# A state-space stage: the products of states take their natural place, and a chunk's state comes ahead of its diagonal products

## The chip, the core and the metric

The kernel runs on one core of one Trainium2 chip. The metric is the device time of that core in microseconds (us), from the first to the last instruction and the little that lies around them. A core has engines that work side by side, each on its own queue, in the order in which the program wrote it: TensorE (PE) multiplies matrices, VectorE (DVE) and ScalarE (ACT) and GpSimd (POOL) work element by element, SyncE (SP) issues transfers. An instruction at the head of a queue that waits for another engine holds up all that stands behind it in that queue.

## What is computed

The reference is two blocks of a network on 512 positions of 1024 channels. The change touches one part of the second block, a state-space mixer. Its input projection gives z, x, B, C and dt; 32 heads of 64 channels stand in 4 groups of 8 heads, and each group goes over 4 chunks of 128 positions, carrying a state from chunk to chunk:

```
def step(state, inp):
    xc, ac, bc, cc = inp
    acum = jnp.cumsum(ac, axis=1)
    seg = jnp.where(causal, acum[:, :, None] - acum[:, None, :], -jnp.inf)
    scores = jnp.einsum('btgn,bsgn->btsg', cc, bc)[..., None] * jnp.exp(seg)
    y_diag = jnp.einsum('btsgh,bsghp->btghp', scores, xc)
    y_off = jnp.einsum('btgn,bghpn->btghp', cc, state) * jnp.exp(acum)[..., None]
    w_end = jnp.exp(acum[:, -1:] - acum)
    new_state = (state * jnp.exp(acum[:, -1])[..., None, None]
                 + jnp.einsum('bsgn,bsghp->bghpn', bc, xc * w_end[..., None]))
    return new_state, y_diag + y_off
```

A gate with z, a norm over each group and the output projection follow. All sums are in fp32.

## The kernel before

The state-space stage lies at about 740 to 1005 us of the span. Its main work is the projections: 128x512 products into PSUM tiles named pa. Operands that need it are split in a rounded part (hi) and a rest (lo), and each product is then three matmuls, hi by hi, hi by lo and lo by hi (mm3, lines 328, 329, 330). These matmuls into pa tiles are called fill here. The scan of a group is woven in among the fill of the next projection; the fourth group stands in the last projection of z, and its end in the output projection.

The scan of group g is the function ssd(g), made of steps on chunks c = 0 to 3:

- rows: two transfers (line 1264, issued by SP, 1 MB each) bring the running sums of the group's eight heads to all partitions, as tiles M.
- scores: four matmuls (line 1243) of B by C, and a copy by ACT (line 1245).
- bt: B is transposed on PE (line 1254) and split in hi and lo (1256 on ACT, 1257 on DVE); C is split too (1248 on ACT, 1249 on POOL).
- decay(i), for each of eight heads: a triangular mask on POOL (line 1272), four exponentials on ACT (1275, one for each chunk), and a product with the scores on DVE (1277). They work on M in place.
- xs(c): four transposes on PE (1284), then on DVE x times dt (1286) and x times D (1287); for c < 3 POOL weighs the former to the end of the chunk (xw, line 1291), ACT rounds it (1248) and POOL forms the rest (1249). The last two are the function parts.
- diag(c): 16 short matmuls (line 1301; the trace has 32 records for them) of M by x, and an addition on DVE (1306).
- state(c), c < 3: three matmuls (328 to 330, into a tile named ps) of B by xw. For c = 0 ACT copies the result (1324); for c > 0 POOL multiplies the old state by its decay (1326) and DVE adds (1328). Then parts splits the new state (1248 on ACT, 1249 on POOL).
- off(c), c > 0: three matmuls (328 to 330, into ps) of C by the parts of state c-1, a product on DVE (1313), an addition on POOL (1315).
- gate, factor, norm, trans: lines 1335, 1340 onwards, 1347, 1353 and 1354.

The matmuls of state, off and diag go to PSUM tiles ps, of which there are four; fill has four pa.

What sets the order on each engine: the program is written as a list of steps s, spread evenly among the steps of the projection by run. A scheduler then orders the instructions of each engine as their operands come free by its own reckoning, and among those that are ready by a priority, which is the place in the program moved forward by a number from the table PRIO. A step is wrapped whole in the priority of its name (L, through at and prio): "state" is 420, "off" is -10, "decay" -860, "xs" -15; the diagonal matmuls have "diag_mm", 3000. The numbers are kept by the change.

## Time and profile before

| | |
|---|---|
| three runs, median (lowest to highest) | 1377.48 us (1375.86 to 1381.73) |
| the profiled execution, its own time | 1378.86 us |
| its span (first to last instruction) | 1377.1 us |
| mean granted TensorE clock, as a share of full speed | 0.988 |
| PE busy | 1316.9 us (96%) |
| DVE, ACT, POOL busy | 862.8 (63%), 659.0 (48%), 311.5 us (23%) |

Busy shares are means over the whole span. A row of the timeline tells when an instruction, or a run of like ones (x and their number), began, how long it lasted, and in brackets how long its engine had been idle just before it and which instruction released it. The matmuls are pipelined: one lasts 0.39 us by its record, while the next begins 0.23 us behind it.

### The profile page before, as it was taken

What the parts mean: (1) busy time and instruction counts of PE and PEld (TensorE: products, weight loads), DVE (VectorE), ACT (ScalarE), POOL (GpSimd) and SP (SyncE); (2) the same over time, 40 slices, a digit from 0 to 9 for tenths busy, and PEclk for the clock granted to TensorE, in tenths of its full rate; (3) what the DMA queues carried; (4) which work ended last, traced back from release to release, by engine and by line L of the source; (5) the groups of instructions that cost most, each with busy time, mean ns of one, the idle gap of its engine ahead of it and who ended that gap; (6) DMA issues with size and microseconds to landing.
All of it is one profiled execution on the core that took longest, in us unless ns stands there. A gap on an engine that the chain in (4) does not pass through costs nothing. (4 is left out here: it accounts for less than half of the span.)

```text
span 1377.1 us, 20584 instructions
## 1 busy us (share of the span) xinstructions
PE 1316.9 (96%) x7927; PEld 1029.5 (75%) x7927; DVE 862.8 (63%) x1260; ACT 659.0 (48%) x1211; POOL 311.5 (23%) x321
## 2 busy tenths in 40 slices
PE   8998999989999999999999999999899999999997
PEld 5773666768888888888778777777688787777776
DVE  5734874294355544422868889677844966777865
ACT  5422464264222223312768465667542835555543
POOL 3532322031000000000202443342400412433421
PEclk9999999999999999999999999999999999999999
DMA  9787663015366654233258354414124354232311
GB/s 298 200 229 209 190 223 101 18 46 185 117 219 214 214 187 135 87 106 118 55 159 278 103 195 149 145 47 161 32 93 138 107 168 123 77 97 72 96 43 61
DMA packets 134733, 189.10 MB, mean 137 GB/s; under 512 B 10280, under 2 KB 95556, under 8 KB 133612
## 3 DMA queue, kind: packets, MB, share of 16 engines
q1 hardware_dynamic: 134588, 187.79, 44.5%
q8 instruction: 62, 1.02, 0.3%
q14 instruction: 35, 0.29, 0.1%
q10 hardware_dynamic: 48, 0.01, 0.0%
HBM read 178.25 MB, written 3.24 MB: 132 GB/s over the span
## 5 line engine op out<-in xcount | busy, mean ns | idle before, releaser
L273 DVE TENSOR_TENSOR wlo<-raw,whi 128x1024 fp32r<-128x1024 f32 (+1 forms) x160 | 208.8, 1316 | 219.2 <-ACT whi L269 209.2
L269 ACT CAST whi<-raw 128x1024 fp32r<-128x1024 f32 (+1 forms) x177 | 182.8, 1046 | 292.2 <-PE pa L329 121.6
L328 PE MATMUL pa<-b,whi 128*128 128x512 f32 x744 | 299.0, 402 | 0.0
L329 PE MATMUL pa<-b,whi 128*128 128x512 f32 x744 | 298.8, 402 | 0.0
L330 PE MATMUL pa<-b,wlo 128*128 128x512 f32 x744 | 297.4, 400 | 0.0
L329 PE MATMUL pa<-wlo,b 128*128 128x512 f32 x424 | 166.6, 393 | 3.4 <-DVE sm L581 3.0
L328 PE MATMUL pa<-whi,b 128*128 128x512 f32 x424 | 166.8, 395 | 1.9 <-ACT b L90 1.5
L330 PE MATMUL pa<-whi,b 128*128 128x512 f32 x424 | 166.1, 393 | 0.0
L328 PEld LDWEIGHTS pa<-b,whi 128*128 128x128 f32 x744 | 140.8, 189 | 32.5 <-issue 6.1
L330 PEld LDWEIGHTS pa<-b,wlo 128*128 128x128 f32 x744 | 140.8, 189 | 31.9 <-issue 1.9
L329 PEld LDWEIGHTS pa<-b,whi 128*128 128x128 f32 x744 | 141.0, 190 | 29.5 <-issue 0.5
L505 DVE SCALAR_TENSOR_TENSOR acc<-raw,c,acc 128x1024 f32<-128x1024 f32 x84 | 118.1, 1406 | 66.4 <-DMA raw<-in_ada_w_dram 44.3
L681 POOL TENSOR_TENSOR b<-w,b 128x512 fp32r<-128x512 f32 x24 | 36.1, 1519 | 469.3 <-DVE sm L586 288.0
L329 PEld LDWEIGHTS pa<-wlo,b 128*128 128x128 f32 x424 | 80.0, 189 | 20.7 <-DVE wlo L273 3.7
L328 PEld LDWEIGHTS pa<-whi,b 128*128 128x128 f32 x424 | 80.2, 189 | 19.2 <-issue 1.8
L330 PEld LDWEIGHTS pa<-whi,b 128*128 128x128 f32 x424 | 79.9, 188 | 17.4 <-issue 0.6
L1457 DVE TENSOR_TENSOR_SCAN w<-w,own 128x512 f32<-128x512 f32 (+3 forms) x64 | 64.1, 1046 | 15.6 <-ACT w L1454 15.6
L1459 POOL TENSOR_TENSOR w<-w,w 128x511 f32<-128x511 f32 (+3 forms) x64 | 67.8, 1063 | 21.8 <-DVE w L1457 20.9
L328 PE MATMUL ps<-whi,b 128*128 128x512 f32 x184 | 72.2, 393 | 0.0
L329 PE MATMUL ps<-wlo,b 128*128 128x512 f32 x184 | 72.1, 392 | 0.0
L330 PE MATMUL ps<-whi,b 128*128 128x512 f32 x184 | 71.9, 391 | 0.0
L777 PE MATMUL ps<-ident,w 128*128 128x128 f32 x240 | 53.5, 283 | 6.1 <-ACT w L787 4.0
(356 smaller groups left out, 2151.8 us busy)
## 6 DMA issues: line engine op xcount, KB each, us to landing
raw<-in_ada_w_dram SPq DMA_DIRECT2D x80, 512.0 KB
raw<-in_w_ffn_in_dram SPq DMA_DIRECT2D x44, 512.0 KB
raw<-in_m_in_w_dram SPq DMA_DIRECT2D x40, 512.0 KB
raw<-in_w_ffn_out_dram SPq DMA_DIRECT2D x22, 512.0 KB
b<-in_ada_w_dram SPq DMA_DIRECT2D x16, 512.0 KB
raw<-in_kv_ada_w_dram SPq DMA_DIRECT2D x16, 512.0 KB
b<-cumd SPq DMA_DIRECT2D x8, 1024.0 KB
raw<-in_m_out_w_dram SPq DMA_DIRECT2D x16, 512.0 KB
```

Source lines behind the costliest of these rows:

```text
L269: nc.scalar.copy(hi[:, :n], u.raw)
L273: eng.tensor_tensor(lo[:, :n], u.raw, hi[:, :n].bitcast(F32), ALU.subtract)
L328: mm(ps, lhsT=lh, rhs=rh, start=first, stop=False)
L329: mm(ps, lhsT=lh, rhs=rl, start=False, stop=False)
L330: mm(ps, lhsT=ll, rhs=rh, start=False, stop=last)
L505: nc.vector.scalar_tensor_tensor(acc, raw, ck, acc, ALU.mult, ALU.add)
L681: nc.gpsimd.tensor_tensor(lo, y[i], hi.bitcast(F32), ALU.subtract)
L777: nc.tensor.transpose(ps[:, (t - s) * P : (t - s + 1) * P], Ps()[e][t][:, s * P : (s + 1) * P], self.ident)
L1457: nc.vector.tensor_tensor_scan(R[:, 0:N][:, ::-1], R[:, 0:N][:, ::-1], self.own[:, S - N : S][:, ::-1], 0.0, ALU.mult, ALU.max)
L1459: nc.gpsimd.tensor_tensor(pr_[:, : N - 1], pr_[:, : N - 1], R[:, 1:N], ALU.mult)
```

## The change

Two things are changed in ssd. First, state and off are no longer wrapped whole in their priority: the PSUM tile and the three matmuls keep the place in which the program writes them, and only what empties the tile (copy or decay, addition, parts for state; product and addition for off) has the priority of that name. Second, the list of steps is written in another order: state(0) stood two places ahead of the end of the decays and now comes behind xs(1); and for each chunk the order is xs(c+1), state(c), diag(c), off(c), where it was xs(c+1), diag(c), off(c), state(c).

```diff
@@ off(c)
                 self.mm3(po, t[:, 2, cs_[c]], t[:, 3, cs_[c]], *box["sp", c - 1], True, True)
-                yo = self.w512()
-                nc.vector.tensor_tensor(r3(yo), r3(po), q(2, c), ALU.mult)
-                y = box["y"][:, c, :]
-                nc.gpsimd.tensor_tensor(y, y, yo, ALU.add)
+                with self.prio("off"):
+                    yo = self.w512()
+                    nc.vector.tensor_tensor(r3(yo), r3(po), q(2, c), ALU.mult)
+                    y = box["y"][:, c, :]
+                    nc.gpsimd.tensor_tensor(y, y, yo, ALU.add)
@@ state(c)
                 self.mm3(pu, t[:, 0, cs_[c]], t[:, 1, cs_[c]], *box["xw", c], True, True)
-                new = box["st", c] = self.w512()
-                box["sp", c] = [self.w512(F32R), self.w512(F32R)]
-                if c == 0:
-                    nc.scalar.copy(new, pu)
-                else:
-                    nc.gpsimd.tensor_tensor(r3(new), r3(box["st", c - 1]), hb(dec[:, 32 * c + 8 * g : 32 * c + 8 * g + 8]),
-                                            ALU.mult)
-                    nc.vector.tensor_tensor(new, pu, new, ALU.add)
-                parts(new, *box["sp", c])
+                with self.prio("state"):
+                    new = box["st", c] = self.w512()
+                    box["sp", c] = [self.w512(F32R), self.w512(F32R)]
+                    if c == 0:
+                        nc.scalar.copy(new, pu)
+                    else:
+                        d = dec[:, 32 * c + 8 * g : 32 * c + 8 * g + 8]
+                        nc.gpsimd.tensor_tensor(r3(new), r3(box["st", c - 1]), hb(d), ALU.mult)
+                        nc.vector.tensor_tensor(new, pu, new, ALU.add)
+                    parts(new, *box["sp", c])
@@ the order of the steps
             L = lambda f, *a: self.at(f.__name__, [lambda: f(*a)])[0]
+            M = lambda f, *a: lambda: f(*a)
             s = [L(rows, 0), L(rows, 1), L(scores), L(bt), L(xs, 0)] + [L(decay, i) for i in range(8)]
-            s.insert(-2, L(state, 0))
+
             for c in range(NT):
                 if c + 1 < NT:
-                    s += [L(xs, c + 1)]
+                    s += [L(xs, c + 1), M(state, c)]
                 s += [L(diag, c)]
                 if c > 0:
-                    s += [L(off, c)]
-                if 0 < c < NT - 1:
-                    s += [L(state, c)]
+                    s += [M(off, c)]
```

No instruction of the four compute engines is added or taken away but two loads of ACT's tables fewer (43 before, 41 after, in the program as it is written). What moves is the order on each engine. Behind line 1310 the line numbers of the changed kernel are up to two or three higher: its copy of state 0 is line 1326, the decay of a state 1329, the addition 1330, the transposes of trans 1355.

The first place is the middle of group 1 on PE, from the transposes of xs(3) on. Before, three products of fill stand between those (tile ps_7328) and the diagonal matmuls of chunk 2 (tile ps_7343):

```order
L1284 MATMUL ps_7328<-ident,b_6623 128x128 x4
L329 MATMUL pa_7406<-b_5508,whi_7203 128x512
L330 MATMUL pa_7406<-b_5506,wlo_7204 128x512
L328 MATMUL pa_7406<-b_5506,whi_7203 128x512
L1301 MATMUL ps_7343<-w_7242,b_6911 64x64 x8
L1301 MATMUL ps_7343<-w_7242,b_6920 64x64 x8
```

After, the three matmuls of state(2) (tile ps_7343, from w_7248 and w_7249, the hi and lo parts of xw) stand ahead of the diagonal ones of chunk 2 (tile ps_7360):

```order
L328 MATMUL pa_7470<-b_5505,whi_7124 128x512
L328 MATMUL ps_7343<-w_7248,b_6947 128x512
L329 MATMUL pa_7470<-b_5507,whi_7124 128x512
L330 MATMUL pa_7470<-b_5505,wlo_7125 128x512
L329 MATMUL ps_7343<-w_7249,b_6947 128x512
L330 MATMUL ps_7343<-w_7248,b_6947 128x512
L328 MATMUL pa_7470<-b_5505,whi_7124 128x512
L329 MATMUL pa_7470<-b_5507,whi_7124 128x512
L330 MATMUL pa_7470<-b_5505,wlo_7125 128x512
L1301 MATMUL ps_7360<-w_7242,b_6911 64x64 x8
L1301 MATMUL ps_7360<-w_7242,b_6920 64x64 x8
```

Before, state(2) came ten products of fill and one of off(2) behind the diagonal matmuls of chunk 2, so that state(2) has moved ahead of those and of some nine products of fill; the matmuls of off(2), which stood around it, now stand by themselves behind the diagonal ones.

The second place is the start of group 3 on PE, where the scores (line 1243) are formed among the last transposes of group 2 (line 1353). Before, they stand among the fill that makes tile pa_8370 from the weights whi_8205:

```order
L330 MATMUL pa_8370<-whi_8205,b_5507 128x512
L1353 MATMUL ps_8326<-ident,b_7740 128x128
L1353 MATMUL ps_8338<-ident,b_7740 128x128
L1243 MATMUL ps_8374<-b_6001 128x128 x4
L1353 MATMUL ps_8338<-ident,b_7740 128x128
L328 MATMUL pa_8370<-whi_8205,b_5505 128x512
```

After, they stand among the fill from the weights whi_8317, the next ones but one:

```order
L1355 MATMUL ps_8326<-ident,b_7740 128x128 x4
L328 MATMUL pa_8359<-whi_8317,b_5506 128x512
L1355 MATMUL ps_8338<-ident,b_7740 128x128
L1243 MATMUL ps_8374<-b_6001 128x128 x4
L1355 MATMUL ps_8338<-ident,b_7740 128x128 x3
L329 MATMUL pa_8359<-wlo_8318,b_5506 128x512
```

The first diagonal matmuls of group 3 stand behind the same product of fill in both orders. Between the scores and them lay 87 products of fill, and now lie 47: the scores moved 40 products back. In the other groups these counts are 111 and 111 (group 0), 105 and 99 (group 1), 115 and 114 (group 2).

The third place is ACT in the same stretch of group 3. Before, the copy of state 0 (line 1324) has five of the group's 32 exponentials behind it:

```order
L1248 CAST w_8414<-w_8412 128x512
L1275 ACTIVATE b_8368<-b_8368,w_6053 128x128 x5
L1324 COPY w_8501<-ps_8497 128x512
L269 CAST whi_8632<-raw_8321 128x1024
L1248 CAST w_8502<-w_8501 128x512
L1275 ACTIVATE b_8368<-b_8368,w_6053 128x128 x5
L1248 CAST w_8552<-w_8550 128x512
L269 CAST whi_8748<-raw_8357 128x1024
L1140 ACT_TABLE_LOAD
```

After, the copy (line 1326) has 24 of the 32 behind it:

```order
L1248 CAST w_8414<-w_8412 128x512
L1275 ACTIVATE b_8363<-b_8363,w_6053 128x128 x6
L1248 CAST w_8539<-w_8537 128x512
L269 CAST whi_8636<-raw_8321 128x1024
L1326 COPY w_8550<-ps_8546 128x512
L1275 ACTIVATE b_8363<-b_8363,w_6053 128x128
L1248 CAST w_8551<-w_8550 128x512
L1275 ACTIVATE b_8363<-b_8363,w_6053 128x128 x7
L1275 ACTIVATE b_8368<-b_8368,w_6053 128x128 x3
L269 CAST whi_8748<-raw_8357 128x1024
L1275 ACTIVATE b_8368<-b_8368,w_6053 128x128 x13
L1140 ACT_TABLE_LOAD
```

What moved is the splitting of xw for chunks 0 and 1 and the state of chunk 0: they stand ahead of most of the exponentials, whose last one the diagonal matmuls of chunk 0 wait for. On SP the transfers of rows of groups 1, 2 and 3 stand behind one, one and three more loads of weights than before.

## Rows read from the trace of the kernel before

**Rows 1.** Page, busy time, share of the span and instructions of each engine:
```profile
PE 1316.9 (96%) x7927; PEld 1029.5 (75%) x7927; DVE 862.8 (63%) x1260; ACT 659.0 (48%) x1211; POOL 311.5 (23%) x321
```

**Rows 2.** Waits of PE, 760 to 1010 us: waited for, total, times, longest:
```profile
PE ps L329 <- POOL w L1249: 5.3, 8, 1.3
PE ps L328 <- ACT w L1248: 4.0, 5, 1.3
```

**Rows 3.** Timeline of PE, groups 0, 1, 2: start, length, instruction, idle before:
```profile
783.65 0.73 PE L328 MATMUL ps<-w,b 128*128 128x512 f32 x2 [0.85 <-ACT w L1248]
785.03 0.50 PE L329 MATMUL ps<-w,b 128*128 128x512 f32 x1 [0.17 <-POOL w L1249]
...
819.73 0.50 PE L329 MATMUL ps<-w,b 128*128 128x512 f32 x1 [0.89 <-POOL w L1249]
...
837.00 1.15 PE L1301 MATMUL ps<-w,b 128*64 128x64 f32 x32 [1.30 <-issue]
...
889.74 0.49 PE L328 MATMUL ps<-w,b 128*128 128x512 f32 x1 [0.41 <-ACT b L1256]
891.52 0.50 PE L329 MATMUL ps<-w,b 128*128 128x512 f32 x1 [1.29 <-POOL w L1249]
...
907.67 1.15 PE L1301 MATMUL ps<-w,b 128*64 128x64 f32 x32
```

**Rows 4.** Timeline of group 0, chunks 1 and 2, on POOL, then ACT, then DVE:
```profile
778.10 1.04 POOL L1291 TENSOR_TENSOR w<-w,w 128x512 f32<-128x512 f32 x1 [3.60 <-PE ps L330]
...
781.13 1.04 POOL L1326 TENSOR_TENSOR w<-w,dec 128x512 f32<-128x512 f32 x1
...
783.68 1.29 POOL L1249 TENSOR_TENSOR w<-w,w 128x512 fp32r<-128x512 f32 x1 [0.27 <-ACT w L1248]
...
782.98 0.62 ACT L1248 CAST w<-w 128x512 fp32r<-128x512 f32 x1 [1.90 <-DVE w L1328]
...
777.34 0.68 DVE L1286 TENSOR_TENSOR w<-ps,w 128x512 f32<-128x512 f32 x1
```

**Rows 5.** Timeline of PE, group 3: scores, fill, first diagonal matmuls, waits behind them:
```profile
944.12 1.06 PE L1243 MATMUL ps<-b 128*128 128x128 f32 x8
...
946.51 0.39 PE L330 MATMUL pa<-whi,b 128*128 128x512 f32 x1
946.74 0.40 PE L328 MATMUL pa<-whi,b 128*128 128x512 f32 x1
...
969.24 1.15 PE L1301 MATMUL ps<-w,b 128*64 128x64 f32 x32 [0.37 <-PE pa L330]
...
976.83 0.50 PE L328 MATMUL pa<-whi,b 128*128 128x512 f32 x1 [1.46 <-ACT b L90]
...
981.75 1.15 PE L1301 MATMUL ps<-w,b 128*64 128x64 f32 x32 [1.44 <-DVE w L1286]
```

**Rows 6.** Timeline of ACT, group 3, from the copy of the scores:
```profile
945.27 0.59 ACT L1245 COPY w<-ps 128x512 f32<-128x512 f32 x1 [0.47 <-PE ps L1243]
945.87 1.28 ACT L1275 ACT_TABLE_LOAD   x1
...
954.60 1.04 ACT L269 CAST whi<-raw 128x1024 fp32r<-128x1024 f32 x1
955.54 3.32 ACT L1275 ACTIVATE b<-b,w 128x128 f32<-128x128 f32 x11
```

**Rows 7.** Timeline of POOL, group 3: rest of C, triangular masks:
```profile
943.95 1.00 POOL L1249 TENSOR_TENSOR b<-b,b 128x384 fp32r<-128x384 f32 x1 [16.40 <-ACT b L1248]
944.90 5.75 POOL L1272 TENSOR_SCALAR_AFFINE_SELECT b<-b 128x512 f32<-128x512 f32 x8
```

**Rows 8.** Timeline of DVE: last products of decays with scores, groups 2 and 3:
```profile
906.88 0.69 DVE L1277 TENSOR_TENSOR b<-b,w 128x512 f32<-128x512 f32 x1 [0.48 <-ACT b L1275]
...
967.01 2.13 DVE L1277 TENSOR_TENSOR b<-b,w 128x512 f32<-128x512 f32 x2
```

**Rows 9.** Stretches: length, busy (number) of PE, PEld, DVE, ACT, POOL, granted clock, DMA:
```profile
760.00:762.00 2.00, 1.53 (x5) 1.21 (x6) 2.00 (x3) 0.59 (x1) 0.41 (x1) 0.72 0.85 229
762.00:764.00 2.00, 2.00 (x6) 1.52 (x6) 1.53 (x3) 1.30 (x2) 1.23 (x1) 0.50 0.20 49
...
978.00:983.00 5.00, 3.16 (x41) 2.10 (x40) 5.00 (x7) 1.25 (x3) 3.71 (x3) 1.00 0.01 3
```

## The prediction, made before the changed kernel ran

> **What bounds the kernel now.** I read the busy shares first: PE is busy for 96% of the span and no other engine for more than 63% [rows 1]. So the kernel gains only where PE stops waiting, and loses only where it waits longer. Then I read PE's waits in the stretch of the state-space stage. Nearly all of them are matmuls of state and off that wait for their operands: 5.3 us for the rest that POOL forms, 8 times, and 4.0 us for the part that ACT rounds, 5 times [rows 2]. That is 9.3 us idle. A wait costs a little more than its idle time, since a record lasts 0.39 to 0.40 us where the next product of fill begins 0.23 us behind [rows 5], so some 0.2 us for each of 13: about 12 us, or 0.9% of the span, is all that a better order of these products can bring. Third I read the timeline of PE around the places that the change moves, and the chain of engines that feeds each.
>
> The chain that feeds a state has a fixed length. In group 0 it is DVE 0.60 us (777.34 to the next), POOL 1.04, ACT 0.62, POOL 1.29 [rows 4]: the hi part is there 2.3 us after DVE begins and the rest 1.3 us later, 3.6 us in all. A product of state is free only where PE has that much other work between the transposes of xs and it. The other chain is longer: the diagonal matmuls of chunk 0 wait for all eight heads' decays, 32 exponentials of 0.30 us on ACT [rows 6] and then a last product on DVE.
>
> **The change part by part.** No matmul is added or removed, so the sum has only waits in it. I count what stands between in the new order, and take durations from the rows.
>
> *Fronts of groups 0 to 2.* Group 0: state(0) has much the same cover as before, and its operands are earlier by one product of 0.6 us on DVE; the diagonal matmuls follow the decays closely, so I take a gain of 0.6 us. Group 1: the idle 0.89 us ahead of state(0) goes, as xw is now weighed between the masks on POOL and not behind all eight; the 1.30 us ahead of the first diagonal matmuls [rows 3] shrink too, since ACT needs about 26 us from the scores to the last exponential (24.0 by adding its instructions in the new order, about 2 waiting), where PE has 99 products and the small ones, about 27.6 us. Together 2.2 us at most; I take 1.7. Group 2: 25 products of fill now stand ahead of state(0), where there were about ten, so its waits of 0.41 and 1.29 us [rows 3], 2.1 us with what a wait costs beside, go. But there the last product of a decay begins at 906.88 us [rows 8] and the diagonal matmuls at 907.67 [rows 3]: no slack. ACT's work between is the same, and only its own wait for state(0) is shorter, so I let 0.7 of the 2.1 us stand. Sum of the three: a gain of 3.0 us, with bounds 0 and 4.9.
>
> *Front of group 3.* The scores move 40 products of fill back while the diagonal matmuls of chunk 0 keep their place. That is 40 x 0.227 = 9.1 us less cover for the decays. Before, 25.1 us passed from the first matmul of the scores at 944.12 to the diagonal matmuls at 969.24, and PE waited 0.37 us ahead of these [rows 5]; from the end of the scores it is 24.1 us, of which 87 x 0.227 = 19.7 is fill and 4.4 all else. After, ACT has to do this between the scores and the last exponential: three copies of 0.59, the rounding of C (0.51), one table load (1.28), 32 exponentials (9.6), the copy of B (0.46), three roundings of 0.62, two casts of weights of 1.04 [rows 6], 17.6 us by the same views. It also waits for POOL where it did not: the first rounding of xw comes behind four masks of 0.72, the rest of C of 1.00 [rows 7] and the weighing of 1.04, some 6.9 us after the scores, where ACT is ready at 4.9; the second costs about 1.3 more, and the first mask 0.4. So ACT is done after 21.3 us, and the last product on DVE, 0.7 us, ends at 22. On PE stand 47 products (10.7), the transposes (1.5), the state (0.7), its own wait for the operands (1.9) and little else: 15 us. **The diagonal matmuls then wait about 7 us** where they waited 0.4. Without the 47 products, 11.3 us of the 22 are not fill, where 4.4 were: a loss of 6.9 us. Bounds: 3 us, if ACT never waits for POOL and the masks run early, and 9 us, if nothing overlaps as I have it.
>
> Behind these three loads of weights on SP stand the rows of group 3. The third load needs a buffer that DVE gives back shortly ahead of the norm of group 2. I take the landing to be hidden, since POOL needs the rows only some 3 us after the scores; if it is not, each us of lateness is one us more of the wait above. Bounds 0 and 5 us, and I take 0.
>
> *Middles of the groups.* Ahead, state(2) stood ten products behind the diagonal matmuls of chunk 2 and its operands were there; off(2) waited for the parts of state 1, as at 783.65 and 785.03 (0.85 and 0.17) [rows 3]. The idle time of this kind was 1.0, 1.1 and 1.6 us in groups 0 to 2 (the same pair of rows in each; group 0 stands here). After, state(2) stands four to six products behind the transposes of xs(3). From the transposes of xs(2) PE has about 2.05 us to the first matmul of state(2) (off(1) 0.7, xs(3) 0.45, four products 0.9), while DVE, POOL and ACT take 2.3 and the hand-overs 0.3: it waits 0.55 us. The rest follows 1.3 us behind, with two products between: 0.6 more. The diagonal matmuls of chunk 2 then need a PSUM tile that DVE empties with the addition of state 1, which waits for POOL's decay of the state, 1.04 us, queued behind the rest of xw: 0.5. Off(2) and off(3) wait 0.5 together. That is 2.2 us for each group; against 3.7 us before, 6.6 in groups 0 to 2, a loss of 2.9. In group 3 the waits of 1.44 us for xs(3) [rows 5] and of some 1.4 us of the usual kind go; 1.46 us for the casts of the output projection [rows 5] stay, and 2.2 come: a gain of 0.6. Sum: a loss of 2.3 us, bounds 0 and 5, or a gain of 3 if the shorter chain of states hides the new waits.
>
> *Sum.* 3.0 - 6.9 - 2.3 = -6.2 us, so 6.2 us slower. The profiled execution took 1378.86 us, which would become 1385.1; the median of the runs is 1377.48, 1.4 us lower, which becomes 1383.7. I forecast **1384 us**.
>
> **The clock.** The row that speaks of it: after the two waits of state(0) in group 0, the granted clock was 0.72 in 760 to 762 us and 0.50, the lower of its two levels, in 762 to 764 [rows 9]. Those four us lost 0.56 + 1.0 us of matmul time, 1.6 in all. But in group 3, PE idled 1.8 of 5 us from 978 to 983, and the clock stayed at 1.00 [rows 9]. So the rows leave open what a wait of 7 us does, and the sum above has nothing for it. The Trainium skill speaks against the change here: its page "TensorE: Matmul & The Clock Gate", section "Why this matters for your kernels", says that a pause between bursts of matmuls sends the engine back to its low clock. By the page the long wait in group 3 would be followed by a stretch at 1.2 GHz, and the sum would be that of rival 2.
>
> **The rivals.**
> 1. *Every wait of state and off goes, and the decays of group 3 are no bound.* For it: these are the waits which the change is aimed at, and in group 2 the cover clearly grows. Against it: the 3.6 us of the chain and the 40 products. It gives 9.3 to 12 us less: 1366 to 1368 us.
> 2. *The forecast with the clock down behind the long wait*: 1.6 us more, 1385.3 us. For it, 760 to 764; against it, 978 to 983.
> 3. *The decays of group 3 are hidden after all*, because ACT and POOL take them faster than in the rows: then fronts and middles remain, +3.0 - 2.3, and the time is 1376.8, no change. It decides below a wait of about 2 us at the diagonal matmuls, that is, if ACT's chain is 17 us and not 22. For it: ACT's instructions alone sum to 17.6. Against it: they are in order, and three of them wait for POOL.
> 4. *The rows of group 3 land late*: up to 5 us more, 1389 us. For it, the load ahead of them that waits for DVE; against it, POOL's 3 us of grace.
>
> That the change does not do what it says is excluded by the new order, where the products of state stand ahead of the diagonal ones in every group.
>
> **How the numbers follow.** The forecast of 1384 has 0.32, rival 2 has 0.22, rival 3 has 0.26, rival 1 has 0.10 and rival 4 has 0.10. The range takes in the forecast, rivals 2 and 3 and most of rival 4, with the bounds of the group 3 front (3 to 9 us): 1374 to 1391 us. This kernel's measurement can tell about 0.5%, 6.9 us, from no change: faster is below 1370.6, slower above 1384.4. Faster is rival 1, 0.10. Slower is rivals 2 and 4 for the most part, 0.27, and the upper half of the forecast, 0.17: 0.44. The rest, 0.46, is no change.
>
> **What would show it.** In the timeline of the changed kernel: the first diagonal matmuls of group 3 idle for some 7 us before, released by DVE's line 1277, and ACT running exponentials until just ahead of it; the first product of state(2) in each group idle 0.5 us for line 1248, the second as much for line 1249; no wait at state(0) of group 2. The granted clock in the 4 us behind the diagonal matmuls of group 3 tells the forecast from rival 2. The prediction is wrong if that long wait is under 2 us, or if state(2) waits nowhere.

## The result: 17 us slower, and the profile after

The changed kernel takes 1394.48 us (median of 4 runs, 1392.16 to 1397.58), beside 1377.43 us for the kernel before in the same series: ratio 1.0122, 95% interval 1.0103 to 1.0140. The forecast was 1384 us with 1374 to 1391 as its range: the sign was right, the size was not. The profiled execution took 1397.58 us, its span is 1395.7 us, its mean granted clock 0.981.

The page, busy times and shares, answers to [rows 1]:

```profile
PE 1325.3 (95%) x7925; PEld 1033.2 (74%) x7927; DVE 865.6 (62%) x1260; ACT 657.0 (47%) x1209; POOL 313.5 (22%) x321
```

The span grew by 18.6 us and PE's busy time by 8.4, though it has no more to do: part of the time is waiting, part is matmuls at a lower clock. PE's waits, 760 to 1010 us, answer to [rows 2] (waited for, total, times, longest):

```profile
PE ps L1301 <- issue: 9.8, 2, 7.3
PE ps L329 <- POOL w L1249: 6.3, 12, 1.3
PE ps L328 <- ACT w L1248: 3.6, 6, 1.0
PE ps L1301 <- DVE b L1277: 3.3, 1, 3.3
```

The waits of state and off (L328, L329), which the change moves, did not shrink: 9.9 us, where they were 9.3. New are 13.1 us ahead of the diagonal matmuls (L1301), where [rows 3, 5] have 1.30 and 0.37. PE's timeline shows where, in groups 0, 1, 2 (with its middle and its transposes) and 3, beside [rows 3] and [rows 5]:

```profile
774.62 1.15 PE L1301 MATMUL ps<-w,b 128*64 128x64 f32 x32 [2.48 <-issue]
...
844.84 1.38 PE L1301 MATMUL ps<-w,b 128*64 128x64 f32 x32 [3.32 <-DVE b L1277]
...
919.65 1.15 PE L1301 MATMUL ps<-w,b 128*64 128x64 f32 x32
...
925.93 0.50 PE L328 MATMUL ps<-w,b 128*128 128x512 f32 x1 [0.51 <-ACT w L1248]
927.29 0.50 PE L329 MATMUL ps<-w,b 128*128 128x512 f32 x1 [0.40 <-POOL w L1249]
929.01 1.15 PE L1301 MATMUL ps<-w,b 128*64 128x64 f32 x32 [0.29 <-DVE w L1330]
931.02 0.50 PE L329 MATMUL ps<-w,b 128*128 128x512 f32 x1 [0.19 <-POOL w L1249]
...
959.38 0.66 PE L1355 MATMUL ps<-ident,b 128*128 128x128 f32 x4 [0.17 <-DVE b L1349]
...
961.62 1.06 PE L1243 MATMUL ps<-b 128*128 128x128 f32 x8
...
984.63 1.98 PE L1301 MATMUL ps<-w,b 128*64 128x64 f32 x32 [7.27 <-issue]
```

The wait in group 3 is the longest, but about half was lost ahead of it. From the first scores of group 0 to the first transposes (trans) of group 2 is 217.8 us (741.57 to 959.38), where it was 198.7 (740.85 to 939.56): 19.1 us more. From there to the first transposes of group 3 is 53.0 us, where it was 55.9. These two lengths, called E and F below, are read in the same way from PE's timeline of every kernel. They sum to 16.2 us more; the other 2.4 us of the span lie outside of them and were not followed.

Fill has moved across the border, and lengths can be compared only net of it. Counted in the two traces between these same milestones, E holds 661 products of fill where it held 611, and F 95 where it held 146. At 0.227 us a product, 11.4 us of E's growth is fill that came in, and F lost 11.6 us of it: net, E grew by 7.7 us and F by 8.7.

What PE did in E and F together, before and then after (length, busy and number of PE, PEld, DVE, ACT, POOL, granted clock, DMA):

```profile
740.85:995.48 254.63, 237.72 (x1634) 188.71 (x1633) 200.92 (x297) 164.37 (x314) 94.67 (x83) 0.99 0.40 128
741.57:1012.38 270.81, 243.97 (x1633) 191.66 (x1631) 200.93 (x297) 162.21 (x312) 95.19 (x83) 0.97 0.38 121
```

PE idles for 26.8 us where it idled for 16.9, 9.9 us more. Most of the rest is the clock.

Stretches at 794, 844, 984 and 994 us answer to [rows 9] (length, busy and number of PE, PEld, DVE, ACT, POOL, granted clock, DMA):

```profile
794.00:796.00 2.00, 1.79 (x5) 1.41 (x6) 0.67 (x2) 0.65 (x1) 1.39 (x2) 0.60 0.82 225
796.00:798.00 2.00, 2.00 (x7) 1.57 (x6) 2.00 (x4) 0.00 (x0) 1.90 (x1) 0.55 0.13 37
...
844.00:846.00 2.00, 1.16 (x32) 1.17 (x32) 1.33 (x3) 0.00 (x0) 0.00 (x0) 0.90 0.83 288
846.00:848.00 2.00, 2.00 (x26) 1.45 (x24) 1.97 (x3) 0.00 (x0) 0.00 (x0) 0.50 0.48 145
848.00:850.00 2.00, 2.00 (x24) 1.75 (x23) 0.75 (x2) 0.72 (x2) 0.00 (x0) 0.75 0.79 246
...
984.00:986.00 2.00, 1.37 (x26) 1.40 (x28) 0.53 (x1) 1.99 (x3) 0.00 (x0) 0.50 0.05 16
986.00:988.00 2.00, 2.00 (x26) 1.45 (x24) 1.25 (x2) 2.00 (x5) 0.00 (x0) 0.50 0.00 0
988.00:990.00 2.00, 2.00 (x31) 1.75 (x27) 0.83 (x2) 0.65 (x2) 0.00 (x0) 0.76 0.00 0
...
994.00:996.00 2.00, 1.11 (x5) 0.72 (x5) 1.59 (x1) 0.56 (x2) 2.00 (x2) 0.94 0.00 0
996.00:998.00 2.00, 2.00 (x16) 1.25 (x16) 1.47 (x3) 0.62 (x1) 0.49 (x1) 0.50 0.00 0
998.00:1000.00 2.00, 2.00 (x29) 1.82 (x27) 1.02 (x2) 0.00 (x0) 2.00 (x2) 0.70 0.00 0
```

Length times what is missing from full speed gives 1.7 us lost behind the wait of 3.32 us, at most 2.5 behind that of 7.27, and 1.7 in each of the other two. Counting only time in which PE was busy, the four sum to 7.3 us. The kernel before had one such place, 760 to 766 us ([rows 9] has its first four us), and lost 1.7. So 5.6 us more go to the clock. Idle time and clock together are 15.5 of the 16.4 us that E and F lost net of fill.

### The profile page after: what moved, and what is told of

Same layout as the page of the kernel before. It is cut to its first block, busy times and chain, and to the rows that moved or that the text cites. A ratio compares the mean times of both kernels' runs of the same rounds, so it can differ in the third digit from the quotient of the medians.

```text
span 1395.7 us, 20586 instructions
## 1 busy us (share of the span) xinstructions
PE 1325.3 (95%) x7925; PEld 1033.2 (74%) x7927; DVE 865.6 (62%) x1260; ACT 657.0 (47%) x1209; POOL 313.5 (22%) x321
## 5 line engine op out<-in xcount | busy, mean ns | idle before, releaser
L328 PE MATMUL pa<-b,whi 128*128 128x512 f32 x744 | 298.9, 402 | 0.9 <-ACT w L1147 0.9
L329 PE MATMUL pa<-b,whi 128*128 128x512 f32 x744 | 298.9, 402 | 0.0
L329 PE MATMUL pa<-wlo,b 128*128 128x512 f32 x424 | 167.5, 395 | 1.2 <-DVE sm L581 0.8
L505 DVE SCALAR_TENSOR_TENSOR acc<-raw,c,acc 128x1024 f32<-128x1024 f32 x84 | 123.7, 1472 | 71.5 <-DMA raw<-in_ada_w_dram 47.9
L328 PE MATMUL pa<-whi,b 128*128 128x512 f32 x424 | 167.2, 396 | 0.1
L328 PEld LDWEIGHTS pa<-b,whi 128*128 128x128 f32 x744 | 140.8, 189 | 33.5 <-issue 5.9
L329 PEld LDWEIGHTS pa<-b,whi 128*128 128x128 f32 x744 | 140.9, 189 | 29.4 <-issue 0.3
L329 PEld LDWEIGHTS pa<-wlo,b 128*128 128x128 f32 x424 | 80.4, 190 | 18.6 <-DVE wlo L273 1.6
L328 PEld LDWEIGHTS pa<-whi,b 128*128 128x128 f32 x424 | 80.2, 189 | 17.4 <-issue 1.4
L1458 DVE TENSOR_TENSOR_SCAN w<-w,own 128x512 f32<-128x512 f32 (+3 forms) x64 | 64.1, 1046 | 15.6 <-ACT w L1455 15.6
L328 PE MATMUL ps<-whi,b 128*128 128x512 f32 x184 | 72.3, 393 | 0.0
L329 PE MATMUL ps<-wlo,b 128*128 128x512 f32 x184 | 72.1, 392 | 0.0
```

Source lines behind the costliest of these rows:

```text
L328: mm(ps, lhsT=lh, rhs=rh, start=first, stop=False)
L329: mm(ps, lhsT=lh, rhs=rl, start=False, stop=False)
L505: nc.vector.scalar_tensor_tensor(acc, raw, ck, acc, ALU.mult, ALU.add)
L1458: nc.vector.tensor_tensor_scan(R[:, 0:N][:, ::-1], R[:, 0:N][:, ::-1], self.own[:, S - N : S][:, ::-1], 0.0, ALU.mult, ALU.max)
```

## The experiments

All were timed in three rounds; each ratio is to the kernel before on the same chip. E and F are from one profiled execution each, and so is what stands behind them: the products of fill in E and in F, PE's idle time in both together, and what the lower clock cost there (half of the time in which PE was busy at the lower level).

| kernel | median us | ratio, 95% interval | E | F | fill in E, F | idle | low clock |
|---|---|---|---|---|---|---|---|
| before | 1377.43 | | 198.7 | 55.9 | 611, 146 | 16.9 | 1.7 |
| split_only | 1379.36 | 1.0006, 0.9997 to 1.0016 | 203.3 | 52.3 | 617, 137 | 15.8 | 3.4 |
| state0_new | 1381.29 | 1.0024, 1.0014 to 1.0033 | 205.5 | 51.4 | 617, 137 | 16.7 | 5.1 |
| split_gate | 1385.22 | 1.0047, 1.0030 to 1.0065 | 201.8 | 59.4 | 610, 149 | 19.4 | 5.1 |
| nowait_before | 1378.25 | 0.9991, 0.9978 to 1.0004 | 196.7 | 56.2 | 597, 156 | 10.9 | 1.7 |
| before_light | 1371.67 | 0.9949, 0.9934 to 0.9963 | 197.2 | 51.6 | 616, 137 | 11.3 | 1.7 |
| after | 1394.48 | 1.0122, 1.0103 to 1.0140 | 217.8 | 53.0 | 661, 95 | 26.8 | 7.3 |
| order_only | 1392.66 | 1.0111, 1.0085 to 1.0137 | 218.2 | 53.2 | 661, 96 | 26.5 | 7.9 |
| state1_ahead | 1396.95 | 1.0123, 1.0098 to 1.0148 | 217.8 | 56.9 | 648, 110 | 26.3 | 11.7 |
| state2_behind | 1396.41 | 1.0127, 1.0104 to 1.0150 | 216.5 | 55.1 | 648, 110 | 27.8 | 7.5 |
| gate_ahead | 1396.86 | 1.0127, 1.0106 to 1.0148 | 217.9 | 56.7 | 650, 106 | 27.8 | 10.5 |
| scores_early | 1397.22 | 1.0138, 1.0114 to 1.0163 | 219.1 | 53.3 | 657, 99 | 27.2 | 8.4 |
| half_exps | 1391.65 | 1.0097, 1.0082 to 1.0112 | 216.8 | 50.6 | 661, 98 | 22.3 | 6.7 |
| bridge | 1391.77 | 1.0094, 1.0077 to 1.0112 | 218.9 | 49.5 | 661, 92 | 19.9 | 3.2 |
| rows_gpsimd | 1395.28 | 1.0116, 1.0092 to 1.0141 | 219.0 | 53.2 | 661, 95 | 27.0 | 8.8 |
| exps_together | 1393.61 | 1.0111, 1.0093 to 1.0130 | 217.8 | 49.2 | 661, 92 | 24.3 | 5.0 |
| nowait_g3 | 1393.03 | 1.0109, 1.0092 to 1.0126 | 219.4 | 51.4 | 661, 93 | 23.4 | 8.2 |
| nowait_after | 1382.93 | 1.0031, 1.0016 to 1.0047 | 203.5 | 55.4 | 597, 158 | 15.6 | 3.4 |
| after_light | 1382.27 | 1.0029, 1.0020 to 1.0039 | 205.9 | 53.5 | 665, 91 | 19.1 | 3.9 |
| light_rows | 1382.35 | 1.0022, 1.0008 to 1.0035 | 205.9 | 53.4 | 665, 91 | 19.7 | 2.8 |

**Which part of the change.** split_only keeps the priorities of after and writes the old order of the steps; order_only writes the new order and wraps state and off whole, as before.

```diff
  split_only, from after
+            s.insert(-2, M(state, 0))
-                    s += [L(xs, c + 1), M(state, c)]
+                    s += [L(xs, c + 1)]
...
+                if 0 < c < NT - 1:
+                    s += [M(state, c)]
```

> Only the first half of the change: state and off are split (matmuls at their natural place, what empties the tile under its priority), the order of the steps stays that of the kernel before. Theory 1 (the order of the steps costs the time, each group's end slips and group 3 pays): the products of fill between scores and first diagonal matmuls are 111, 106, 114 as before and 67 in group 3 with 20 more behind, so 1377 to 1383 us, and at most 3 us of wait ahead of group 3's diagonal matmuls. Theory 2 (the lost early place of the state products costs it): 1388 us or more, with the waits for lines 1248 and 1249 as in the changed kernel.

> Only the second half of the change: the new order of the steps, with state and off whole in their priority as before. Theory 1: as slow as the changed kernel, 1391 to 1397 us, with a wait of 6 to 8 us ahead of group 3's first diagonal matmuls (47 products of fill from the scores to them) and waits of 2 us or more ahead of those of groups 0 and 1. Theory 2: 1383 us or less.

The order is the cause: 1379.36 us without it, 1392.66 with it alone (ratios 1.0006 and 1.0111).

**Which state.** state2_behind puts only state(2) back behind off(2); state0_new is split_only with state(0) at its new place; state1_ahead is split_only with state(1) alone ahead of diag(1). (In the words on state1_ahead, state(2) stands behind off(2), as in the kernel before.)

```diff
  state1_ahead, from split_only
                     s += [L(xs, c + 1)]
+                if c == 1:
+                    s += [M(state, 1)]
...
-                if 0 < c < NT - 1:
+                if c == 2:
                     s += [M(state, c)]
```

> The changed kernel, but state(2) stands behind diag(2) and off(2) again, as before the change; state(0) and state(1) stay ahead of their chunk's diagonal matmuls. Covers 111, 106, 116 and 60. The new waits at the first product of state(2), at its rest and at the PSUM tile of diag(2), about 1.2 us a group in the changed kernel, go; group 3's wait falls by 13 products, 3 us, to 4.3 us, and group 1's by 1.4 us. Theory: 1384 to 1388 us. Rival (state(0) and state(1) cost it): 1392 us or more.

> The old order with whole steps' products kept in their place (as in split_only), and one thing of the new order alone: state(0) stands behind xs(1) and ahead of diag(0); state(1) and state(2) stay behind the off steps. Theory S1 (it is state(1) ahead of diag(1) that lengthens a group, since the product fills of a group then end later and the next group's scores slip): nothing of the slip here, 1379 to 1382 us, no long wait of L1301 in group 3 (under 2 us) since the scores stand at 2913 products of fill as in the kernel before. Theory S0 (state(0)'s place makes the long waits of groups 0 and 3): 1385 to 1392 us, with a wait of 2 us or more at the first diagonal matmuls of group 0 and of 5 us or more in group 3.

> The old order with one thing of the new order alone: state(1) stands ahead of diag(1), state(2) ahead of off(2) as in the kernel before's order of off(1) and so on; state(0) stays ahead of the last two decays. By its program the scores of group 3 stand 27 products of fill later than in the kernel before, and the fill between scores and first diagonal matmuls of group 3 is 60 products, as in state2_behind. Theory S1 (state(1)'s place is the cause): 1393 to 1397 us, as state2_behind (1396.4), with a wait of 3.5 to 5 us in group 3. Theory S0 (state(0)'s place is the cause): 1379 to 1384 us, and no wait over 2 us ahead of any group's diagonal matmuls.

My theory on state(2) fell: 1396.41 us. **One step makes the loss: state(1) ahead of diag(1)**, 1396.95 us against 1379.36 for split_only, which differs in that alone. state(0) costs some 2 us (1381.29; ratios 1.0024 and 1.0006).

**What makes the wait in group 3.** Seven kernels take something from that front, or show what lies behind it. scores_early gives the scores a pa tile, so that they go 40 products earlier. half_exps leaves out the exponentials of the last four heads of group 3, and fills the masked places of these heads with 0 (not in the cut below). gate_ahead puts the priority of the gates from -180 to 0, split_gate does the same to split_only. bridge puts seven matmuls ahead of the diagonal ones in group 3, each reading a head's decays as they come; they cost time of their own, and show the clock. rows_gpsimd and exps_together are described in their expectations.

```diff
  scores_early
-                ps = self.psum()
+                ps = self.psum("pa" if g == 3 else "ps")
  half_exps
-                for c, cs in enumerate(cs_):
+                for c, cs in enumerate(cs_ if g < 3 or i < 4 else []):
  bridge, in diag
+                if g == 3 and c == 0:
+                    for i in range(7):
+                        nc.tensor.matmul(py, lhsT=box["M", i // 4][:, i % 4, 0:P], rhs=box["xdt", 0], start=True, stop=True)
  rows_gpsimd
-                nc.sync.dma_start(box["M", i].rearrange("p a b -> p (a b)"),
+                (nc.gpsimd if g == 3 else nc.sync).dma_start(box["M", i].rearrange("p a b -> p (a b)"),
  exps_together, around the mask and the exponentials
+                with (self.tc.high_priority(1860) if g == 3 else nullcontext()):
```

> The changed kernel, but the scores of group 3 go to a PSUM tile of the other pool, so that they stand 40 products of fill earlier (87 to the diagonal matmuls, as before the change); the transfers of rows and the exponentials keep their place. Theory A (the prediction's step: the place of the scores takes the cover away): the wait of 7.3 us ahead of group 3's diagonal matmuls falls under 1 us and the time to 1385 us. Theory B (the exponentials begin late because the rows are issued late on SP, at 958.5 us, behind three more loads, and the scores only stand beside that): the wait stays 6 to 8 us and the time 1392 to 1397 us.

> The changed kernel without the exponentials of the last four heads of group 3 (their scores are multiplied by the masked rows as they are): 16 activations of 0.30 us fewer on ACT, 4.8 us, ahead of group 3's first diagonal matmuls; the rest of the order nearly as in the changed kernel. If ACT's chain sets those matmuls: the wait of 7.3 us falls to 1.5 to 2.7 us, the granted clock behind it stays at 1.00, and the time is 1387 to 1390 us. If the rows' landing or POOL's masks set it: the wait stays over 5 us and the time over 1392 us.

> The changed kernel with one number of the table changed: the priority of the gates from -180 to 0, so that on DVE the gates of a group no longer stand behind the next group's convolution taps (lines 1150, 12 of them and 8.0 us from 939.5 us on in the changed kernel). The middles of the groups keep their order; between scores and first diagonal matmuls stand 111, 117, 116 and 59 products of fill where the changed kernel has 111, 100, 115 and 47. Theory (a group's end slips behind other work on DVE, and the next group's decays begin late): group 1's wait of 3.3 us goes (17 products, 3.9 us more cover), group 3's 7.3 us falls to about 4.5, and the time to 1384 to 1389 us. Rival (the middles with their new waits cost the time): 1392 us or more.

> The first half of the change alone (order of the steps as before) with the gates' priority at 0. Covers 111, 107, 114 and 84 and no wait of more than 1.3 us ahead of any group's diagonal matmuls. Theory: between 1374 and 1380 us, since the waits of state and off are as before and nothing else is gained; under 1374 us would show that the place of the gates costs the kernel before too.

> The changed kernel with seven more matmuls (128 by 512, their output is overwritten) ahead of group 3's first diagonal ones, each of which reads one head's decays as soon as they are done, so that PE works now and then during the wait of 7.3 us; the diagonal matmuls still wait for the last head. If the pause lowers the clock: the granted clock stays above 0.9 there, the 32 records of a chunk's diagonal matmuls take 1.15 us and not 1.98, and the time is about 2 us lower, 1391 to 1394 us. If the clock falls for another reason: 0.50 behind the wait as before and no gain.

> The kernel after, with the two loads of group 3's rows (L1264) issued from GpSimd's queue, which stands idle from 941.4 to 964.3 us there, in place of SyncE's, where they stand behind five weight loads and go out at 958.5 us. Scores, diagonal matmuls and the fill between them (47 products) keep their places. Theory R (the rows, held up behind the weight loads, set the exponentials of group 3): rows are issued at about 942 us, the first exponential starts at 946 to 950 in place of 965.9, the wait of 7.3 us at the first diagonal matmuls falls under 2 us, the low clock behind it goes, and the time is 1383 to 1388 us. Theory A (ScalarE's copies and casts hold the exponentials up whenever the rows come): the wait stays at 4 us or more, 1391 to 1396 us.

> rows_gpsimd (1395.3), with group 3's masks and exponentials given a priority of 1000 in place of -860: on GpSimd all eight masks stand ahead of the C parts, on ScalarE all 32 exponentials stand in one row behind the casts of B and C, ahead of the casts of the chunk's parts, which then come about 10 us later. Theory T (the late exponentials alone make the wait): exponentials end at about 975 us in place of 983.7, the wait at the first diagonal matmuls falls from 7.75 to under 2.5 us and the time to 1387 to 1391 us. Theory C (ScalarE's queue has no slack there: what is gained at the diagonal matmuls is lost at the state's products, which wait for the casts): the wait falls, but new waits of 3 us and more stand at L328 and L329 behind L1248 and L1249, and the time stays 1393 to 1397 us.

With the scores 40 products earlier the wait stayed at 5.79 us, so their place was not its main cause. Without half the exponentials it fell to 3.25 us, so ScalarE's chain makes much of it; that is more than the 2.7 us expected, and the clock fell behind it all the same (0.50 from 978 to 984 us). In rows_gpsimd (POOL, POOL, ACT, PE) the rows went out 20 us earlier than in the kernel after (938.41 for 958.52), for nothing:

```profile
938.41 1.25 POOL L1264 DMA_DIRECT2D b<-cumd  x2
961.36 1.01 POOL L1249 TENSOR_TENSOR b<-b,b 128x384 fp32r<-128x384 f32 x1 [21.70 <-ACT b L1248]
...
965.28 1.28 ACT L1275 ACT_TABLE_LOAD   x1
...
982.14 1.98 PE L1301 MATMUL ps<-w,b 128*64 128x64 f32 x32 [7.75 <-issue]
```

The masks stand in POOL's queue behind the rest of C (L1249), which waits for ACT's rounding of C (L1248), and that stands behind the copies of group 2's transposes. exps_together puts masks and exponentials together behind that. Its timeline, ACT then PE:

```profile
966.82 9.48 ACT L1276 ACTIVATE b<-b,w 128x128 f32<-128x128 f32 x32
976.20 0.61 ACT L1248 CAST w<-w 128x512 fp32r<-128x512 f32 x1
...
976.86 0.50 PE L328 MATMUL ps<-w,b 128*128 128x512 f32 x1 [3.20 <-ACT w L1248]
977.29 1.96 PE L1302 MATMUL ps<-w,b 128*64 128x64 f32 x32
...
988.27 0.50 PE L328 MATMUL ps<-w,b 128*128 128x512 f32 x1 [2.15 <-ACT w L1248]
```

The wait of 7 us is gone from the diagonal matmuls, and 3.20 and 2.15 us stand at the states, which wait for ACT's roundings behind the exponentials. F is 3.8 us shorter, the median 1 us; theories T and C each had a part. gate_ahead moved waits in the same way: 4.04 us in group 3, but 27.8 us of idle time in all, for 26.8. In split_gate the same number made the old order slower, 1385.22 us for 1379.36, against what was expected; why was not followed. bridge kept the granted clock at 1.00 where it was 0.50; two of its stretches:

```profile
968.00:970.00 2.00, 1.74 (x7) 1.43 (x8) 0.75 (x1) 0.61 (x3) 2.00 (x3) 1.00 0.00 0
970.00:972.00 2.00, 1.39 (x4) 0.33 (x2) 0.10 (x1) 1.70 (x3) 2.00 (x4) 1.00 0.00 0
```

It is 2.7 us faster than after, which fits what the clock cost there (2.2 us behind the wait and 1.7 at 994 us, by the trace of after), less what the seven matmuls cost; the two intervals just overlap. None of these brings back the 17 us, and the table says why: E is 216 to 220 us in all of these that start from after, and by its end 650 to 661 products of fill are used up, for 611. Group 3 then has little fill left to wait behind.

**The hold.** One line makes the first diagonal matmul wait for the last head's decay. Three kernels go without it: the kernel before, the kernel after, and the kernel after in group 3 alone.

```diff
-                            if i == t == 0 and c == 0:
-                                self.wait(m.ins, box["decayed"].ins)
```

> The kernel before, without the line that holds diag(0) until the last head's decay is done: the diagonal matmuls of chunk 0 go as each head's decay comes, spread among the fill. It is the base for nowait_after. The hold costs 0.4 us at group 3 and 1.3 us of low clock at group 1 there; matmuls of 36 ns each that come alone may cost more than in a row. 1374 to 1386 us.

> The kernel after without the same line. What counts is nowait_after less nowait_before, against 17 us with the line. Theory R (late rows in group 3): the last heads' matmuls still come late, but one after the other with fill between, so that half of group 3's 11 us goes: a difference of 8 to 14 us. Theory H (it is the hold, which turns a late last head into a wait of PE and a low clock): the difference falls under 5 us.

> The kernel after, with the hold of diag(0) for the last head's decay left out in group 3 alone. Theory H3 (the hold costs where it stands ahead of group 3's late exponentials, as the 10.6 us left in after_light less before_light say): 1383 to 1388 us, no low clock behind 970 us. Theory H0 (the gain of nowait_after is in groups 0 to 2, whose fronts it moved by 40 to 70 products of fill): 1391 to 1396 us.

Without the hold the new order costs 4.7 us (1382.93 less 1378.25), not 17 (theory H), and E differs by 6.8 us at the same fill (597), F by -0.8. So a loss in E stays, and that of group 3 is gone. In group 3 alone, leaving the hold out does nearly nothing (1393.03): theory H0. So most of the price needs both, state(1) ahead of diag(1) and diagonal matmuls that all come behind the last decay. By these counts it is made in groups 0 to 2, where the hold and the new order together use up fill; net of fill, about half of it is then paid in group 3.

**VectorE's weight sums.** These sums (L503, L505) stand in VectorE's queue among the scan. after_light and before_light cut them and their loads from 1024 columns to 64, so that most of them is left out; light_rows adds rows_gpsimd to after_light. In the kernel after, the last products of group 1's decays (L1277) stand behind such a sum, which waits for its load:

```profile
840.55 1.28 DVE L505 SCALAR_TENSOR_TENSOR acc<-raw,c,acc 128x1024 f32<-128x1024 f32 x1 [1.17 <-DMA raw<-in_ada_w_dram]
...
842.89 1.89 DVE L1277 TENSOR_TENSOR b<-b,w 128x512 f32<-128x512 f32 x3
```

The edit, one line of it:

```diff
-                    nc.vector.scalar_tensor_tensor(acc, raw, ck, acc, ALU.mult, ALU.add)
+                    nc.vector.scalar_tensor_tensor(acc[:, s], raw[:, s], ck, acc[:, s], ALU.mult, ALU.add)
```

> The kernel before, with the adaLN sums of this stage (L503 and L505, 128x1024 each) and their loads cut to 64 of 1024 columns, so that part of the computation is left out. It is the base for after_light. The sums are VectorE's 1.28 us each beside a PE that is 95% busy, so both theories expect little here: 1370 to 1380 us.

> The kernel after, with the same cut as before_light (the sums and their loads only 64 columns wide). What counts is after_light less before_light, against 17 us between the whole kernels. Theory D (VectorE's in-order queue: the mask products of groups 0 and 1 stand behind an L505 that waits for its load, 1.17 us at 840 us): the difference falls to 9 to 12 us, and the wait of 3.3 us at the first diagonal matmuls of group 1 falls under 1 us. Theory O (the order itself: ScalarE's exponentials come too late for the fill that is left, whatever VectorE does): the difference stays 14 to 19 us, with the wait of group 3 at 6 us or more.

> after_light (the weight sums of this stage and their loads only 64 of 1024 columns wide) with the rows of group 3 issued from GpSimd's queue as in rows_gpsimd. If the two causes found (VectorE's sums in groups 0 and 1, SyncE's queue ahead of group 3) are the whole of the 17 us, little is left against before_light (1371.7): 1371 to 1376 us, no wait over 2 us ahead of any diagonal matmuls. If there is a third cost in the order, 1378 to 1382 us.

The difference falls from 17 to 10.6 us (1382.27 less 1371.67), and the waits at the diagonal matmuls of groups 0 and 1 go from 2.48 and 3.32 us to none and 0.34. That is theory D for these two groups. Group 3 of after_light still has its wait, and that is what is left of the difference: E has 49 products more than in before_light and grew by 8.7 us, less than these products take, while F has 46 fewer and grew by 1.8. So a light VectorE does not mend the order, and earlier rows on top of it gain nothing (light_rows, 1382.35):

```profile
831.51 1.15 PE L1305 MATMUL ps<-w,b 128*64 128x64 f32 x32 [0.34 <-issue]
...
970.74 1.55 PE L1305 MATMUL ps<-w,b 128*64 128x64 f32 x24 [8.62 <-issue]
```

**The tail of a group in the trace.** From the first diagonal matmuls of a group to its first transposes, groups 0 to 2 took 29.6, 35.9 and 31.9 us before, and 35.8, 41.7 and 39.7 after. In group 2 of state0_new, which has state(1) at its old place, DVE does this after diagonal matmuls at 911.87:

```profile
916.83 0.68 DVE L1314 TENSOR_TENSOR w<-ps,w 128x512 f32<-128x512 f32 x1
920.49 0.69 DVE L1330 TENSOR_TENSOR w<-ps,w 128x512 f32<-128x512 f32 x1 [0.94 <-POOL w L1329]
924.20 0.68 DVE L1314 TENSOR_TENSOR w<-ps,w 128x512 f32<-128x512 f32 x1
...
929.61 0.69 DVE L1314 TENSOR_TENSOR w<-ps,w 128x512 f32<-128x512 f32 x1 [1.61 <-PE ps L330]
...
936.68 0.68 DVE L1337 TENSOR_TENSOR b<-b,b 128x512 f32<-128x512 f32 x1
```

And in the kernel after, behind diagonal matmuls at 919.65:

```profile
928.27 0.69 DVE L1330 TENSOR_TENSOR w<-ps,w 128x512 f32<-128x512 f32 x1 [3.57 <-POOL w L1329]
928.88 0.68 DVE L1314 TENSOR_TENSOR w<-ps,w 128x512 f32<-128x512 f32 x1
...
938.12 1.28 DVE L1314 TENSOR_TENSOR w<-ps,w 128x512 f32<-128x512 f32 x2
939.53 7.98 DVE L1150 SCALAR_TENSOR_TENSOR w<-pa,m_conv_w,w 128x511 f32<-128x511 f32 x12
...
953.63 0.68 DVE L1337 TENSOR_TENSOR b<-b,b 128x512 f32<-128x512 f32 x1
```

The product of off(1) (L1314) came 5.0 us behind the first diagonal matmuls; now it stands in DVE's queue behind the addition of state 1 (L1330), which waits 3.57 us for POOL's decay of the old state, and comes at 9.2. The products of off(2) and off(3) come at 18.5 and 19.1 us for 12.3 and 17.7, and the last gate (L1337) at 34.0 for 24.8, with 12 taps of the convolution ahead of the gates. These three tails hold 55 products of fill more (10, 17 and 28; 12.5 us). So the longer chain costs PE little at once, 2.8 us of idle time more in the three tails: it takes in fill, of which 40 products are then missing between the scores and the diagonal matmuls of group 3. Gates ahead of taps (gate_ahead) did not shorten E, so the taps are not the cause by themselves. That the place of L1314 behind L1330 lengthens the tails is read from the traces; no run moved that one instruction.

## Why the prediction was wrong

Net of fill at 0.227 us a product, the stage lost 16.4 us (E and F) where the sum had 6.2. **Two steps failed: the clock, for which the sum had nothing, and the fronts of groups 0 to 2, taken as a gain.** Step by step, with the low clock taken out of each stretch and counted by itself:

- **The clock: 0.** This step failed first. Measured: a loss of 5.6 us more than before, 7.3 for 1.7. The sum had nothing for it because the rows left it open; the row for it, 978 to 983, has 1.8 us of idle time in 5 and a clock of 1.00, and the changed kernel has four places where the clock fell. Two lie behind the long waits of groups 1 and 3, two behind short waits of state or off (L328, L329). Rival 2 had the mechanism in one place and a price of 1.6; by the sign named for it, the clock of 0.50 behind the wait of group 3, it came true there.
- **Fronts of groups 0 to 2: gain 3.0.** This step failed too. Measured: a loss of 2.0 us, or of 0.3 if the clock that fell in group 0's front before is counted in (scores to diagonal matmuls +0.2, +0.6 and -1.6 us; by the traces 106 products of fill became 100 in group 1, and 114 became 115 in group 2). Group 2 gained 1.8, more than my 0.7. In groups 0 and 1 I took DVE to be ready, and the waits were 2.48 and 3.32 us. In group 1 DVE stood at an L505 that waits for its load, with the last masks' products behind it (840.55, 1.17 us idle); in group 0 these stood behind an L505 and a split of weights of 2.31 us each. after_light took both waits away.
- **Front of group 3: loss 6.9.** Measured: 7.0 (2.1 us shorter, with 40 products or 9.1 us less fill); the wait was 7.27 us for "about 7". The size was right. The reason was half right: that the exponentials end late is so, but not because the scores stood late in PE's order (scores_early). All of group 2 ends late, and the copies, roundings and masks of group 3 queue behind that.
- **Middles of the groups: loss 2.3 (2.9, less 0.6 in group 3).** Measured from the first diagonal matmuls to the first transposes: the tails of groups 0 to 2 lost 7.4 us (19.9 longer, 12.5 of it fill), that of group 3 lost 1.7. Of these 9.1 us, 7.3 are the clock, and 1.9 remain. The waits came as I had them or smaller (in group 2 0.51, 0.40, 0.29 and 0.19 for 0.55, 0.6, 0.5 and 0.5). What I did not follow was the chain on DVE and POOL to the gates and transposes that end a group; it lengthens the tails by the fill that they take in.
- **Rival 4, late rows:** they were late (issued at 958.52 for 932.36 us), and it cost next to nothing (rows_gpsimd). Rivals 1 and 3 did not happen.

So of the missing 10.2 us, 5.6 are the clock and 5.0 the fronts, less 0.4 in the middles. These figures are from one execution of each kernel, that of after the slowest of its four, and the clock differs: 5.0 to 11.7 us in those with the new place of state(1), the hold and the whole sums, but 3.2 in bridge; 1.7 to 5.1 in those of the old order. No version here that computes the same beats the kernel before: nowait_before is within its interval (0.9978 to 1.0004).

## What to carry to other kernels

When matmuls are moved ahead, follow what empties their PSUM tiles, too: here the new evacuation stood ahead of an older one in VectorE's queue, and as it waited for GpSimd, what stood behind it came late. Cost a stage by two sums, the engine's idle time and what a lower clock takes behind the waits, and ask of each new wait what the clock does behind it. A longer chain on other engines costs TensorE little while there is fill to cover it (2.8 us of idle time in three tails here); count how much is left for the last group. To place a loss, use lengths between milestones, and count the filler between the same two points: the raw E and F put the whole loss ahead of group 3, net of fill it is half. The longest wait does not place it either.

## What was unexpected of the hardware

A wait of 3.32 us at the diagonal matmuls of group 1 was followed by the lower level of the clock (0.50 from 846 to 848 us, with PE busy throughout); one of 1.30 us at the same place in the kernel before was not (1.00 from 836 to 844). But the clock also fell behind two short waits with two matmuls between them, of 0.38 us ahead of 792.17 and 1.31 us ahead of 794.21 (after, 0.60 and 0.55 in the next 4 us). The lower level also came without one long wait: in nowait_g3 PE was busy for 1.1 of the 4 us from 986 to 990, in pieces, and the clock was 0.56 and 0.58 in the 4 us behind. That a pause is followed by matmuls at the low level is what the Trainium skill says, on its page "TensorE: Matmul & The Clock Gate", section "Why this matters for your kernels"; the trace of after agrees in group 3 (0.50 behind 7.27 us), and bridge, which filled that pause with matmuls, stayed at 1.00.
